# One split per q and k for both heads of a pair, with moves inside SBUF to the halves' partitions

## The chip, the core and the metric

The kernel runs on one core of a Trainium2 chip. The metric is the device time of one execution in microseconds (us); the time before is the median of three runs. The core's engines are TensorE (PE, whose weight loads are listed as PEld), VectorE (DVE), ScalarE (ACT), GpSimd (POOL) and SyncE (SP, which here issues the DMAs). Each works through its own queue in order and waits there for semaphores.

## The reference

Two decoder layers on x of 512 tokens by 1024, 16 heads of 64; layer 0 attends by stick-breaking, layer 1 by softmax with a forget gate, and each is followed by a gated MLP with a causal convolution of width 3. Cut to what matters here:

```python
for i in range(2):
    mod = silu(c) @ w_mod[i] + b_mod[i]          # six vectors: shift, scale, gate, twice
    h = rmsnorm(x, g_mix_pre[i]) * (1 + sc_a) + sh_a
    q, k, v = split_heads(h @ w_qkv[i])          # 16 heads of 64
    if i % 2 == 0:                               # strictly causal, s < t
        z = q @ k.T / 8
        a[t, s] = sigmoid(z[t, s]) * prod(1 - sigmoid(z[t, j]) for s < j < t)
    else:                                        # causal, s <= t
        a = softmax(q @ k.T / 8 + sum(log_sigmoid(f_j) for s < j <= t))
    x = x + gt_a * rmsnorm((a @ v) @ w_o[i], g_mix_post[i])
    h = rmsnorm(x, g_ffn_pre[i]) * (1 + sc_f) + sh_f
    y = (silu(conv3(h @ w_gate[i])) * (h @ w_up[i])) @ w_down[i]
    x = x + gt_f * rmsnorm(y, g_ffn_post[i])
```

## The kernel before

Everything is float32, and each matmul operand is kept as two parts: `hi`, the value rounded to the matmul's float32r format, and `lo`, what the rounding left. A product is three matmuls, hi by hi, hi by lo and lo by hi (`mm3`, lines 266 to 268, in the order ah by bh, ah by bl, al by bh). A split is a copy to hi on ACT (line 192) and a subtraction on DVE or POOL (line 193).

An attention layer works on pairs of heads, 0 to 7. `proj` makes one pair's q (j = 0) or k (j = 1): 24 matmuls into one PSUM bank with head A of the pair on partitions 0 to 63 and head B on 64 to 127. It is a generator that yields after every three matmuls; such a step is called a group here. `queries` then makes two tiles, qa and qb: qa has A's hi on rows 0 to 63 and A's lo on rows 64 to 127; qb has B's hi on 64 to 127 and B's lo on 0 to 63. Each takes one ACT and one DVE operation on 64 partitions. `keys` makes for each head a tile kh with its hi on both halves and a tile kl with its lo on its own half and zeros on the other (a fill on POOL). Per head that is an ACT copy, a POOL copy to the other half, a DVE subtraction and the fill. Two matmuls then give the three products of a score (`scores`, line 380), and since the contraction always runs over 128 rows the zeros are needed.

`attention` goes through the 16 heads. For a head it writes four score blocks and their softmax or stick-breaking (`fox`: fx, cum; `stick`: bt, om), and for the head before the transposes (pa, then ah and al) and the product with v (po). Between these it runs other matmul groups from a list, `gens`, so many per head as the table `UNITS` says: the projections of pairs 1 to 7 in order, q then k; after an even pair the four v blocks of the next two pairs (`values`, tile pv, two weight tiles of four d each); last the first products with w_o (`project`, tile po, by pair p). The PE and SP queues are in program order. The orders on ACT, DVE and POOL outside layer 0's start are set by the framework's scheduler from its own estimates, and they are fixed before the run.

Weights come through `Stream`: `need` at a projection's start also issues the next tiles, two ahead. A tile is loaded to wf (three buffers), copied to wh on ACT and subtracted to wl on POOL (three buffers each). So the load of tile i + 2 is written in SP's queue at the start of projection i, behind all that was written there before, and a DMA whose semaphore isn't there yet holds up those behind it. In layer 0, `bg.step` writes up to three loads of w_mod (tile wm) at the end of a head; DVE sums them into acc (line 143). In layer 1 each head loads a tile cum.

Of the kernel before, what the change touches and what calls it, by code (L numbers as in the profile page):

```python
# [8 lines left out]
F32 = mybir.dt.float32  # L9
F32R = mybir.dt.float32r  # L10
BF16 = mybir.dt.bfloat16
AF = mybir.ActivationFunctionType
ALU = mybir.AluOpType
AX = mybir.AxisListType

P = 128
D = 1024
S = 512
# [19 lines left out]
def trunk(ctx, tc, x, c, w_mod, b_mod, g_mix_pre, g_mix_post, w_qkv, w_o, w_fg, b_fg,  # L38
          g_ffn_pre, g_ffn_post, w_gate, w_up, w_conv, b_conv, w_down, out):
    nc = tc.nc  # L40
    cst = ctx.enter_context(tc.tile_pool(name="cst", bufs=1))
    sb = ctx.enter_context(tc.tile_pool(name="sb", bufs=1))
# [4 lines left out]
    def nm(s):  # L47
        serial[0] += 1
        return f"{s}_{serial[0]}"

    def bank(s="b"):
        return pp.tile([P, 512], F32, tag="bank", name=nm(s), bufs=8)

    def slot(s, dt=F32R):
        return sb.tile([P, 512], dt, tag="slot", name=nm(s), bufs=NS)

    def t2(s):
        return sb.tile([P, 512], F32, tag="t2", name=nm(s), bufs=4)

    def t4(s, dt=F32):  # L60
        return sb.tile([P, D], dt, tag="t4", name=nm(s), bufs=3)
# [25 lines left out]
    xs = cst.tile([P, NT, D], F32, name="xs")  # L87
    csil = cst.tile([P, ND], F32, name="csil")
    rowsA, rowsB, rowsC = t2("rowsA"), t2("rowsB"), t2("rowsC")
    nc.sync.dma_start(rowsC[:ND, :P], c.rearrange("b (r p) -> (b r) p", p=P))  # L90
    nc.scalar.dma_start(rowsA[:96, :P], b_mod.rearrange("l (r p) -> (l r) p", p=P))
# [23 lines left out]
    def conv_columns():  # L115
        ps = bank("pcol")
        for l in range(DEPTH):
            nc.tensor.transpose(ps[:, P * l : P * l + 88], rowsB[:88, P * l : P * l + P], idn[:88, :88])
        for l in range(DEPTH):
            nc.vector.tensor_copy(colB[l], ps[:, P * l : P * l + 88])  # L120
        yield
# [69 lines left out]
    def split(hi, lo, src, engine=None):  # L191
        nc.scalar.copy(hi, src)  # L192
        (engine or nc.vector).tensor_tensor(lo, src, hi.bitcast(F32), op=ALU.subtract)  # L193
# [70 lines left out]
    def mm3(ps, lhs, rhs, first, last):  # L264
        (ah, al), (bh, bl) = lhs, rhs
        nc.tensor.matmul(ps, ah, bh, start=first, stop=False)  # L266
        nc.tensor.matmul(ps, ah, bl, start=False, stop=False)  # L267
        nc.tensor.matmul(ps, al, bh, start=False, stop=last)  # L268
# [21 lines left out]
    def new_ht():  # L290
        hi = sb.tile([P, ND, S], F32R, tag="hth", name=nm("hth"), bufs=1)
        lo = sb.tile([P, ND, S], F32R, tag="htl", name=nm("htl"), bufs=1)
        return hi, lo

    def block(ht, d, c0, c1):
        return ht[0][:, d, c0:c1], ht[1][:, d, c0:c1]
# [15 lines left out]
    def modulated(t, xn, ht, gcol, shcol):  # L312

        ts_ = slice(t * P, (t + 1) * P)
        for h in range(2):
            ps = bank("pt")
            for j in range(4):
                d = 4 * h + j
                nc.tensor.transpose(ps[:, j * P : (j + 1) * P], xn[h][:, j * P : (j + 1) * P], idn)
            hf = t2("hf")  # L320
            for j in range(4):
                d = 4 * h + j
                js = slice(j * P, (j + 1) * P)
                nc.scalar.activation(hf[:, js], ps[:, js], AF.Identity, scale=gcol[:, d : d + 1], bias=shcol[:, d : d + 1])
            hi, lo = (x_[:, 4 * h : 4 * h + 4, ts_] for x_ in ht)
            hf = hf.rearrange("p (b k) -> p b k", b=4)
            (nc.scalar.copy if h else nc.vector.tensor_copy)(hi, hf)
            nc.vector.tensor_tensor(lo, hf, hi.bitcast(F32), op=ALU.subtract)  # L328

    def postnorm(t, banks, gt):  # L330
        ms, us = [square(b) for b in banks], []
        for h in range(2):
            us.append(t2("u"))
            nc.vector.tensor_tensor(us[h], banks[h], gt[:, 512 * h : 512 * h + 512], op=ALU.mult)
        r = rstd(ms)
        for h in range(2):
            x_ = xs[:, t, 512 * h : 512 * h + 512]
            nc.vector.scalar_tensor_tensor(x_, us[h], r, x_, op0=ALU.mult, op1=ALU.add)


    def proj(l, p, j, ht, scale, res, parts=((0, S),)):
        wh, wl = ws.need((l, "qk", p, j))
        ps = bank("pqk")
        for c0, c1 in parts:
            for d in range(ND):
                ds_ = slice(d * P, (d + 1) * P)
                mm3(ps[:, c0:c1], (wh[:, ds_], wl[:, ds_]), block(ht, d, c0, c1), d == 0, d == ND - 1)
                if c1 - c0 == S or d % 2:
                    yield
        res[p, j] = queries(ps, scale) if j == 0 else keys(ps)  # L350

    A, B = slice(0, HD), slice(HD, P)

    def queries(ps, scale):

        res = slot("qa"), slot("qb")
        for x_, own, other in ((res[0], A, B), (res[1], B, A)):
            nc.scalar.activation(x_[own], ps[own], AF.Copy, scale=scale)
            nc.vector.scalar_tensor_tensor(x_[other], ps[own], scale, x_[own].bitcast(F32), op0=ALU.mult, op1=ALU.subtract)
        return res  # L360

    def keys(ps):


        res = []
        for own, other in ((A, B), (B, A)):
            hi, lo = slot("kh"), slot("kl")
            nc.gpsimd.memset(lo.bitcast(F32)[other], 0.0)
            nc.scalar.copy(hi[own], ps[own])
            nc.gpsimd.tensor_scalar(hi[other], hi[own].bitcast(F32), 1.0, 1.0, op0=ALU.mult, op1=ALU.mult)  # L370
            nc.vector.tensor_tensor(lo[own], ps[own], hi[own].bitcast(F32), op=ALU.subtract)
            res.append((hi, lo))
        return res

    def scores(l, hd, qb, q, k):
# [65 lines left out]
    def values(l, g, t, ht, vt):  # L441

        w = [ws.need((l, "v", g, i), 2 - i) for i in range(2)]
        ps = bank("pv")
        for d in range(ND):
            c = slice(256 * (d % 4), 256 * (d % 4) + 256)
            mm3(ps[:, :256], block(ht, d, t * P, (t + 1) * P), (w[d // 4][0][:, c], w[d // 4][1][:, c]), d == 0, d == ND - 1)
            if d % 2:
                yield
        keep_values(ps[:, :256], g, t, vt)  # L450
# [109 lines left out]
    def begin(vt, qk):  # L560
# [169 lines left out]
        for j in range(ND):  # L730
# [16 lines left out]
            for i in order[lead:]:  # L747
                multiply(j, i)
        qk[0, 0] = queries(acc[4], 0.125)
        qk[0, 1] = keys(acc[6])  # L750
        ws.upto(1)
        for g in range(2):
# [6 lines left out]
    for l in range(DEPTH):  # L759
        bg = Background([(l, GT_A), (l, SC_F), (l, SH_F)] if l == 0 else [])  # L760
        scale = -0.125 if l % 2 else 0.125
        vt, qk = {}, {}
        if l == 0:
            with tc.manual_schedule(engines={mybir.EngineType.Activation, mybir.EngineType.DVE, mybir.EngineType.Pool}):
                ht = begin(vt, qk)
            conv_rows()
        else:
            drain(values(l, 0, 0, ht, vt))
            ready(2)
            drain(values(l, 0, 1, ht, vt))  # L770
            first = proj(l, 0, 0, ht, scale, qk, ((0, 256), (256, 512)))
            for _ in range(4):
                next(first)
            ready(3)
            drain(values(l, 0, 2, ht, vt))
            if l % 2:
                cums_of[l] = forget(ht)
            drain(values(l, 0, 3, ht, vt))
            drain(first)
            drain(proj(l, 0, 1, ht, None, qk))  # L780
# [11 lines left out]
                    mm3(banks[t][h], (ot[p][0][:, ts_], ot[p][1][:, ts_]), w[h], p == 0, p == NPAIR - 1)  # L792
                    yield

        gens, ot = [], []
        for p in range(1, NPAIR):
            if (l, p) == (0, 3):
                gens.append(conv_columns())
            gens += [proj(l, p, j, ht, s, qk) for j, s in ((0, scale), (1, None)) if (p, j) not in qk]
            if p % 2 == 0 and (p // 2, 0) not in vt:  # L800
                gens += [values(l, p // 2, t, ht, vt) for t in range(NT)]
        gens += [project(t, ps_) for ps_ in (range(3), range(3, 5)) for t in range(2)] + [project(2, range(3))]
# [6 lines left out]
        ht = new_ht()  # L809
# [77 lines left out]
        if not last:  # L887
            ht = new_ht()
# [47 lines left out]
```

## Time and profile before

| what | value |
|---|---|
| median of 3 runs | 1315.79 us (1315.13 to 1317.24) |
| the profiled execution, its own time | 1318.06 us |
| its span, first to last instruction | 1316.3 us |
| granted TensorE clock, mean | 0.994 |
| PE, DVE, ACT, POOL busy | 1249.9, 839.5, 617.8, 292.7 us |
| layer 0's attention | about 75 to 285 us |
| layer 1's attention | about 690 to 905 us |

Rows of groups read: line, engine, operation, result<-sources with partitions by elements, count | busy time, mean ns of one | idle time of the engine ahead of them and what ended it. Rows in order of time read: start in us, duration in us, engine (SPq is the DMA issue queue of SP), line, operation, and in brackets the idle time before. Rows of waits read: who, for whom, us in total, times, the longest. Rows of DMA issues end with the median us from issue to landing. Rows of stretches read: from and to, length, busy us of each engine with its count of instructions, clock, busy share of the 16 DMA engines, GB/s.

### The profile page before, as it was taken

Reading aid. Unit: us, or ns where it says so; the run is one execution under the profiler, and the core shown is the slowest. Engines: PE = TensorE matmul, PEld = TensorE weight load, DVE = VectorE, ACT = ScalarE, POOL = GpSimd, SP = SyncE. Lnnn points to the kernel's source line nnn. Section 1 sums busy time; section 2 is a strip of 40 time slices with the busy share of each in tenths; the row PEclk is TensorE's granted clock in tenths of the full one; section 3 lists DMA queues with packets and bytes.
Section 4 is the critical chain, followed back from the end, with each engine's and each line's share of the span. In section 5 each row is a group of like instructions: output and inputs, shape, how many; then the busy total and the mean of one; then the engine's idle time right before and its main releaser. Section 6 shows DMA issues by size and latency. Waiting matters only on the chain.

```text
span 1316.3 us, 17089 instructions
## 1 busy us (share of the span) xinstructions
PE 1249.9 (95%) x6244; PEld 1047.3 (80%) x6244; DVE 839.5 (64%) x1455; ACT 617.8 (47%) x1182; POOL 292.7 (22%) x326
## 2 busy tenths in 40 slices
PE   4887978999999999999999899999999999999997
PEld 3676956878888788888888789887898888888886
DVE  7979899757869898532345677786776444443233
ACT  5465655657434343321346556666753333332121
POOL 3575454641000000000032745454100000000000
PEclk9999999999999999999999999999999999999999
DMA  8653343222658777333411533432254333333221
GB/s 272 196 164 109 115 157 129 65 80 64 215 159 272 220 227 238 108 96 97 144 50 32 180 109 94 119 112 81 80 177 134 99 100 98 97 97 96 96 96 64
DMA packets 174856, 169.19 MB, mean 129 GB/s; under 512 B 6936, under 2 KB 151728, under 8 KB 174772
## 3 DMA queue, kind: packets, MB, share of 16 engines
q1 hardware_dynamic: 174596, 168.04, 41.0%
q8 instruction: 49, 0.80, 0.2%
q14 instruction: 35, 0.29, 0.1%
q10 hardware_dynamic: 176, 0.07, 0.0%
HBM read 165.92 MB, written 2.16 MB: 128 GB/s over the span
## 4 chain that ended last, share of the span: by engine, by line
PE 67%; DVE 18%; ACT 6%; DMA 4%; issue 4%; POOL 1%; SPq 1%; DVEq 0%; POOLq 0%; ACTq 0%
PE pgu L267 11%; PE pgu L268 11%; PE pgu L266 11%; PE pd L266 6%; PE pd L268 6%; PE pd L267 6%; PE pqk L266 2%; DVE om L389 2%; PE pqk L267 2%; PE pqk L268 2%; DVE acc L143 2%; PE ps L380 2%; DVE bt L390 1%; ACT junk L287 1%; PE pa L412 1%
## 5 line engine op out<-in xcount | busy, mean ns | idle before, releaser
L192 ACT CAST wh<-wf 128x1024 fp32r<-128x1024 f32 (+2 forms) x178 | 185.0, 1039 | 308.7 <-PE pd L268 134.8
L193 DVE TENSOR_TENSOR wl<-wf,wh 128x1024 fp32r<-128x1024 f32 x122 | 149.3, 1224 | 216.8 <-ACT wh L192 214.6
L267 PE MATMUL pgu<-htl,wh 128*128 128x512 f32 (+1 forms) x736 | 276.4, 376 | 0.3 <-DVE htl L328 0.2
L266 PE MATMUL pgu<-hth,wh 128*128 128x512 f32 (+1 forms) x736 | 276.4, 375 | 0.0
L268 PE MATMUL pgu<-hth,wl 128*128 128x512 f32 (+1 forms) x736 | 276.2, 375 | 0.0
L193 POOL TENSOR_TENSOR wl<-wf,wh 128x1024 fp32r<-128x1024 f32 (+3 forms) x56 | 135.2, 2418 | 230.8 <-ACT wh L192 218.6
L267 PEld LDWEIGHTS pgu<-htl,wh 128*128 128x128 f32 x736 | 138.5, 188 | 25.8 <-DVE htl L328 0.7
L266 PEld LDWEIGHTS pgu<-hth,wh 128*128 128x128 f32 x736 | 138.5, 188 | 25.0
L268 PEld LDWEIGHTS pgu<-hth,wl 128*128 128x128 f32 x736 | 138.5, 188 | 24.9
L279 POOL TENSOR_TENSOR r<-v,mhalf 128x1 f32<-128x1 f32 x32 | 17.8, 555 | 450.7 <-DVE v L275 450.7
L268 PE MATMUL pd<-wh,yl 128*128 128x512 f32 x288 | 112.0, 389 | 0.0
L266 PE MATMUL pd<-wh,yh 128*128 128x512 f32 x288 | 112.0, 389 | 0.0
L267 PE MATMUL pd<-wl,yh 128*128 128x512 f32 x288 | 112.0, 389 | 0.0
L143 DVE SCALAR_TENSOR_TENSOR acc<-wm,csil,acc 128x1024 f32<-128x1024 f32 x74 | 100.4, 1357 | 15.2 <-DMA wm<-in_w_mod_dram 14.6
L266 PE MATMUL pqk<-hth,wh 128*128 128x512 f32 (+1 forms) x240 | 100.6, 419 | 0.0
L268 PE MATMUL pqk<-hth,wl 128*128 128x512 f32 (+1 forms) x240 | 93.4, 389 | 1.1 <-POOL wl L193 1.1
L267 PE MATMUL pqk<-htl,wh 128*128 128x512 f32 (+1 forms) x240 | 93.4, 389 | 0.0
L848 ACT ACTIVATE cv<-cv 128x512 f32<-128x512 f32 x44 | 27.8, 632 | 106.1 <-DVE cv L847 100.7
L266 PE MATMUL pv<-wh,hth 128*128 128x256 f32 (+1 forms) x224 | 70.4, 314 | 0.3
L268 PE MATMUL pv<-wh,htl 128*128 128x256 f32 (+1 forms) x224 | 67.6, 302 | 1.2 <-DVE htl L662 1.0
L267 PE MATMUL pv<-wl,hth 128*128 128x256 f32 (+1 forms) x224 | 67.3, 300 | 0.0
L849 DVE TENSOR_TENSOR cv<-cv,pgu 128x512 f32<-128x512 f32 x44 | 30.2, 686 | 51.8 <-PE pgu L268 45.7
(193 smaller groups left out, 2518.6 us busy)
## 6 DMA issues: line engine op xcount, KB each, us to landing
wm<-in_w_mod_dram SPq DMA_DIRECT2D x80, 512.0 KB, 5.1
wf<-in_w_ffn_gate_dram SPq DMA_DIRECT2D x44, 512.0 KB, 4.4
wf<-in_w_ffn_up_dram SPq DMA_DIRECT2D x44, 512.0 KB, 3.6
wf<-in_w_ffn_down_dram SPq DMA_DIRECT2D x44, 512.0 KB, 3.5
wf<-in_w_qkv_dram SPq DMA_DIRECT2D x41, 512.0 KB, 3.7
wm<-in_w_mod_dram SPq DMA_DIRECT2D x32, 256.0 KB, 4.0
wf<-in_w_o_dram SPq DMA_DIRECT2D x16, 512.0 KB, 3.5
cum<-cumd SPq DMA_DIRECT2D x16, 512.0 KB, 4.3
```

Source lines behind the costliest of these rows:

```text
L143: nc.vector.scalar_tensor_tensor(acc, w, csil[:, d : d + 1], acc, op0=ALU.mult, op1=ALU.add)
L192: nc.scalar.copy(hi, src)
L193: (engine or nc.vector).tensor_tensor(lo, src, hi.bitcast(F32), op=ALU.subtract)
L266: nc.tensor.matmul(ps, ah, bh, start=first, stop=False)
L267: nc.tensor.matmul(ps, ah, bl, start=False, stop=False)
L268: nc.tensor.matmul(ps, al, bh, start=False, stop=last)
L279: nc.gpsimd.tensor_tensor(r, v, mhalf, op=ALU.pow)
L287: nc.scalar.activation(junk(), src, AF.Square, scale=1.0 / 32.0, accum_out=m)
L380: nc.tensor.matmul(ps[:, :n], q[hd][:, qs], k[hd][i][:, :n], start=i == 0, stop=i == 1)
L389: nc.vector.tensor_tensor_scan(om[:, :n][:, ::-1], ps[:, :n][:, ::-1], zid[:, S - n :][:, ::-1], 0.0, op0=ALU.mult, op1=ALU.add)
L848: nc.scalar.activation(a, a, AF.Silu)
L849: nc.vector.tensor_tensor(a, a, u, op=ALU.mult)
```

## The change

For pairs 1 to 7 (in layer 0 the q of pair 1 was made before) a q or k is split once for both heads, on all 128 partitions, into two tiles hi and lo of the four-buffer kind t2. Then DMAs on SP's queue bring their halves into place: for k six (hi to both halves of each kh, lo to the own half of each kl), for q four. The zero halves of kl are filled once per layer, in two pairs of tiles that pairs use in turn (`low_rooms`). `queries` and `keys` stay for pair 0 and for what layer 0's start makes.

```diff
-    def t2(s):
-        return sb.tile([P, 512], F32, tag="t2", name=nm(s), bufs=4)
+    def t2(s, dt=F32):
+        return sb.tile([P, 512], dt, tag="t2", name=nm(s), bufs=4)
...
-    def proj(l, p, j, ht, scale, res, parts=((0, S),)):
+    def proj(l, p, j, ht, scale, res, parts=((0, S),), kl=None):
...
-        res[p, j] = queries(ps, scale) if j == 0 else keys(ps)
+        if p:
+            res[p, j] = placed(ps, scale, kl[p % 2] if j else None)
+        else:
+            res[p, j] = queries(ps, scale) if j == 0 else keys(ps)
...
+    def placed(ps, scale, kl):
+        hi, lo = t2("hi", F32R), t2("lo", F32R)
+        def place(dst, src):
+            nc.sync.dma_start(dst.bitcast(F32), src.bitcast(F32))
+        if kl:
+            split(hi, lo, ps)
+            res = [(slot("kh"), kl[0]), (slot("kh"), kl[1])]
+            for own, (h_, l_) in zip((A, B), res):
+                place(h_[A], hi[own])
+                place(h_[B], hi[own])
+                place(l_[own], lo[own])
+        else:
+            nc.scalar.activation(hi, ps, AF.Copy, scale=scale)
+            nc.vector.scalar_tensor_tensor(lo, ps, scale, hi.bitcast(F32), op0=ALU.mult, op1=ALU.subtract)
+            res = slot("qa"), slot("qb")
+            for x_, own, other in ((res[0], A, B), (res[1], B, A)):
+                place(x_[own], hi[own])
+                place(x_[other], lo[own])
+        return res
+
+    def low_rooms():
+        res = []
+        for _ in range(2):
+            res.append((slot("kl"), slot("kl")))
+            for x_, other in zip(res[-1], (B, A)):
+                nc.gpsimd.memset(x_.bitcast(F32)[other], 0.0)
+        return res
...
-        gens, ot = [], []
+        gens, ot, kl = [], [], low_rooms()
...
-            gens += [proj(l, p, j, ht, s, qk) for j, s in ((0, scale), (1, None)) if (p, j) not in qk]
+            gens += [proj(l, p, j, ht, s, qk, kl=kl) for j, s in ((0, scale), (1, None)) if (p, j) not in qk]
```

The order of PE's instructions is the same before and after. Lines behind `proj` move down by 36. Three places show what else moves.

SP's queue at the end of layer 1's attention, before (w_o tiles o0 to o4 in order, and cum of the heads):

```order
L198 DMA wf_8556<-in_w_o_dram 128x1024
L490 DMA cum_8586<-cumd 128x1024
L198 DMA wf_8679<-in_w_o_dram 128x1024
L490 DMA cum_8718<-cumd 128x1024
L198 DMA wf_8784<-in_w_o_dram 128x1024
L198 DMA wf_8825<-in_w_o_dram 128x1024
```

The same place after (qa, qb and kh, kl are pair 7's; wf_8747 is o1, wf_8852 is o2):

```order
L384 DMA qa_8741<-lo_8738 64x512
L384 DMA qb_8742<-hi_8737 64x512
L384 DMA qb_8742<-lo_8738 64x512
L198 DMA wf_8747<-in_w_o_dram 128x1024
L526 DMA cum_8786<-cumd 128x1024
L384 DMA kh_8842<-hi_8838 64x512 x2
L384 DMA kl_6714<-lo_8839 64x512
L384 DMA kh_8843<-hi_8838 64x512 x2
L384 DMA kl_6715<-lo_8839 64x512
L198 DMA wf_8852<-in_w_o_dram 128x1024
L198 DMA wf_8893<-in_w_o_dram 128x1024
```

The loads of o2 and of the tiles after it now stand behind the six moves of pair 7's k, and that of o1 behind the four of its q. The same holds in layer 0.

SP's queue at the v weights of pairs 4 and 5 in layer 1 (two tiles of 128x4x256), before:

```order
L198 DMA wf_7358<-in_w_qkv_dram 128x8x128
L198 DMA wf_7447<-in_w_qkv_dram 128x4x256
L490 DMA cum_7468<-cumd 128x1024
L198 DMA wf_7564<-in_w_qkv_dram 128x4x256
L490 DMA cum_7607<-cumd 128x1024
```

After (qa and qb are pair 4's):

```order
L198 DMA wf_7499<-in_w_qkv_dram 128x4x256
L526 DMA cum_7520<-cumd 128x1024
L384 DMA qa_7614<-hi_7610 64x512
L384 DMA qa_7614<-lo_7611 64x512
L384 DMA qb_7615<-hi_7610 64x512
L384 DMA qb_7615<-lo_7611 64x512
L198 DMA wf_7620<-in_w_qkv_dram 128x4x256
```

The second v tile now stands behind the moves of the q that was projected just before it; it is so at all five places of this kind, two in layer 0 and three in layer 1.

DVE's queue in heads 0 and 1 of layer 0, before (om and bt of head 0, kl of pair 1, acc of w_mod):

```order
L390 TENSOR_TENSOR bt_872<-bt_872,om_873 128x127
L371 TENSOR_TENSOR kl_895<-pqk_839,kh_894 64x512
L143 SCALAR_TENSOR_TENSOR acc_1176<-wm_1179,csil,acc_1176 128x1024
L371 TENSOR_TENSOR kl_901<-pqk_839,kh_900 64x512
L389 SCALAR_TENSOR_TENSOR om_923<-ps_919,zid 128x512
L193 TENSOR_TENSOR al_938<-pa_932,ah_937 128x512
L143 SCALAR_TENSOR_TENSOR acc_1176<-wm_1182,csil,acc_1176 128x1024
L389 SCALAR_TENSOR_TENSOR om_948<-ps_944,zid 128x384
L193 TENSOR_TENSOR al_962<-pa_957,ah_961 128x384
L143 SCALAR_TENSOR_TENSOR acc_1176<-wm_1185,csil,acc_1176 128x1024
```

After, from head 0's first om on:

```order
L425 SCALAR_TENSOR_TENSOR om_835<-ps_831,zid 128x512
L193 TENSOR_TENSOR lo_903<-pqk_847,hi_902 128x512
L425 SCALAR_TENSOR_TENSOR om_855<-ps_851,zid 128x384
L425 SCALAR_TENSOR_TENSOR om_868<-ps_864,zid 128x256
L426 TENSOR_TENSOR bt_867<-bt_867,om_868 128x255
L425 SCALAR_TENSOR_TENSOR om_881<-ps_877,zid 128x128
L426 TENSOR_TENSOR bt_880<-bt_880,om_881 128x127
L425 SCALAR_TENSOR_TENSOR om_931<-ps_927,zid 128x512
L193 TENSOR_TENSOR al_946<-pa_940,ah_945 128x512
L425 SCALAR_TENSOR_TENSOR om_956<-ps_952,zid 128x384
L193 TENSOR_TENSOR al_970<-pa_965,ah_969 128x384
L395 SCALAR_TENSOR_TENSOR lo_1014<-pqk_920,hi_1013 128x512
```

One subtraction (lo) stands for the two kl, and the acc steps are gone from here: the first eight stood in heads 0 to 2 and now stand in heads 3 to 5, where w_mod's loads have come behind the moves in SP's queue.

## The prediction

> **What bounds the kernel now.** I read the page first, then stretches of time over the two attention stages (the only stages the diff touches), then the waits in them, then single rows at the places where the DMA queue's order changes.
>
> ```profile
> span 1316.3 us, 17089 instructions
> ```
>
> ```profile
> core 0: us, PE busy (x) PEld busy (x) DVE busy (x) ACT busy (x) POOL busy (x), PEclk, DMA share, GB/s
> 75.00:128.00 53.00, 43.45 (x208) 34.30 (x207) 47.03 (x67) 33.45 (x73) 31.61 (x40) 0.97 0.48 151
> 128.00:180.00 52.00, 46.19 (x279) 40.42 (x279) 47.72 (x68) 31.02 (x70) 26.24 (x38) 0.97 0.41 132
> 180.00:260.00 80.00, 70.21 (x392) 58.98 (x391) 70.77 (x130) 49.24 (x108) 41.04 (x56) 0.98 0.31 100
> ...
> 690.00:905.00 215.00, 207.27 (x1242) 179.19 (x1241) 157.21 (x392) 135.33 (x315) 108.12 (x96) 1.00 0.35 106
> ```
>
> The first three stretches are layer 0's attention (185 us). There PE idles 185 - 159.9 = 25.1 us while DVE is busy for 165.5 us, 89%: DVE is the bound. The last stretch is layer 1's attention: PE is busy for 96% and DVE for 73%. There PE is the bound, so each us that PE waits is a us of the run. The waits of layer 0 (75 to 260 us) agree, and the DMA queue's own (60 to 300 us) show that one waiting issue holds all behind it:
>
> ```profile
> PE ps L380 <- DVE om L389: 9.6, 5, 5.1
> ...
> SPq L139 <- PE pm L161: 28.4, 1, 28.4
> ```
>
> **The work that goes.** These groups are from 75 to 260 us:
>
> ```profile
> L371 DVE TENSOR_TENSOR kl<-pqk,kh 64x512 fp32r<-64x512 f32 x14 | 9.6, 683 | 2.1 <-ACT kh L369 1.9
> L193 DVE TENSOR_TENSOR al<-pa,ah 128x512 fp32r<-128x512 f32 x13 | 8.7, 671 | 0.1
> L369 ACT CAST kh<-pqk 64x512 fp32r<-64x512 f32 x14 | 8.1, 580 | 20.6 <-DVE kl L371 20.6
> L192 ACT CAST ah<-pa 128x512 fp32r<-128x512 f32 x13 | 7.7, 590 | 0.0
> L359 DVE SCALAR_TENSOR_TENSOR qb<-pqk,qb 64x512 fp32r<-64x512 f32 x6 | 4.2, 693 | 2.1 <-ACT qb L358 2.0
> L359 DVE SCALAR_TENSOR_TENSOR qa<-pqk,qa 64x512 fp32r<-64x512 f32 x6 | 4.1, 685 | 1.8 <-ACT qa L358 1.6
> ```
>
> An operation on 128 partitions costs what one on 64 does (671 beside 683 ns on DVE, 590 beside 580 on ACT). So each pair's k and each q lose one DVE and one ACT operation, and their one copy and one subtraction no longer take turns (ACT's 20.6 us of waiting for DVE at kh).
>
> Layer 0, DVE: 7 k by 0.683 and 6 q by 0.69 = 8.9 us of busy time, and of the 1.9 + 2.0 + 1.6 = 5.5 us in which DVE waited for ACT about half, 2.7. The upper bound is 11.6 us. The lower is 3, for DVE's order is new too (eight acc steps of heads 0 to 2 move to heads 3 to 5, where they make DVE full). I take **-8**. ACT (13 by 0.58) and POOL (two copies and, but for the four fills of a layer, two fills less per k) are cover, not path: nothing for them. Layer 1 (7 q, 7 k) sheds the same from engines that aren't the bound: **-1**, between 0 and -2.
>
> **What is added: transfers in SP's queue.** Per k six moves of 128 KB, per q four: 7 by 6 + 6 by 4 in layer 0 and 7 by 10 in layer 1, 136 in all. The trace has no move inside SBUF; the nearest rows are
>
> ```profile
> wf<-in_w_qkv_dram SPq DMA_DIRECT2D x41, 512.0 KB, 3.7
> wf<-in_w_o_dram SPq DMA_DIRECT2D x16, 512.0 KB, 3.5
> out_dram<-xs SPq DMA_DIRECT2D x8, 256.0 KB, 2.0
> ```
>
> so about 2 us to land, from 1 (half the bytes) to 3.5. Their own landing is mostly covered: scores read a pair's q and k one to three heads later, except pair 7. What isn't covered is SP's order. SP reaches a weight load only after the moves written ahead of it have been issued, and these wait for hi (ACT) and lo (DVE) of the projection that has just ended. Before, SP ran far ahead of PE. Where the load is used 16 matmul groups later (16 us), the delay is hidden. It isn't in two kinds of place.
>
> **Third o tile (o2), used four groups after pair 7's k.** Layer 1 before:
>
> ```profile
> 869.87 0.33 SPq L198 DMA_DIRECT2D wf<-in_w_o_dram  x1
> 884.90 1.05 ACT L192 CAST wh<-wf 128x1024 fp32r<-128x1024 f32 x1
> 886.42 2.40 POOL L193 TENSOR_TENSOR wl<-wf,wh 128x1024 fp32r<-128x1024 f32 x1
> 889.02 0.40 PE L267 MATMUL po<-wl,oh 128*128 128x512 f32 x1
> ...
> 842.32 0.49 DVE L402 TENSOR_SCALAR fx<-fx,rc 128x512 f32<-128x512 f32 x1
> ...
> 887.31 1.80 DVE L402 TENSOR_SCALAR fx<-fx,rc 128x512 f32<-128x512 f32 x1
> 890.28 0.67 DVE L371 TENSOR_TENSOR kl<-pqk,kh 64x512 fp32r<-64x512 f32 x1
> ```
>
> The load was issued 19 us before use, its split began when pair 7's projection freed the buffer, and wl was ready at 888.82 for a matmul at 889.02: no slack. Now the load stands behind pair 7's moves. DVE's lo has the place of the kl row, done at 890.95; then four issues (kl, kh twice, kl) by 0.37 = 1.5, the load 3.5, the cast 1.05, wl 2.40: 899.4, 10.4 us after the matmul wants it. The fx row ahead of kl took 1.80 us while that wl ran on POOL, and 0.49 at 842.32 with no wl beside it; with wl gone from there lo is 1.3 earlier: **+9**. The least is hi and lo at once after the projection's end (884.9, when the wh row began): 884.9 + 0.59 + 0.67 + 1.5 + 6.95 = 894.6, +5.6; the most +10.4 and a later landing, +12. The Trainium skill, "SBUF — State Buffer", section "Who interferes with whom", says that a DVE operation in its two-port mode and GpSimd lock each other out of a shared port for a whole instruction. The two fx rows agree with it; without it the term would be +10.4.
>
> Layer 0 before:
>
> ```profile
> 256.34 2.29 DVE L390 TENSOR_TENSOR bt<-bt,om 128x127 f32<-128x127 f32 x1
> ...
> 258.63 0.67 DVE L371 TENSOR_TENSOR kl<-pqk,kh 64x512 fp32r<-64x512 f32 x1
> ...
> 261.85 0.39 PE L267 MATMUL po<-wl,oh 128*128 128x512 f32 x1
> ```
>
> 259.3 + 1.5 + 6.95 = 267.75 against 261.85: 5.9. The 2.29 us bt again lay beside o2's wl; lo comes up to 1.9 earlier: **+4** (from 2 to 7). Head 14's wait for its moved kh (2 us after lo) lies inside this stall.
>
> **Second v tile, used ten groups after a q.** Layer 1's three, with SP's issue of one of these loads, the q row whose place lo takes, and the first matmul that reads wl of the second tile:
>
> ```profile
> 774.43 0.37 SPq L198 DMA_DIRECT2D wf<-in_w_qkv_dram  x1
> 748.30 0.68 DVE L359 SCALAR_TENSOR_TENSOR qa<-pqk,qa 64x512 fp32r<-64x512 f32 x1 [0.61 <-ACT qa L358]
> 755.09 0.28 PE L267 MATMUL pv<-wl,hth 128*128 128x256 f32 x1
> 798.60 0.68 DVE L359 SCALAR_TENSOR_TENSOR qa<-pqk,qa 64x512 fp32r<-64x512 f32 x1
> 804.50 0.28 PE L267 MATMUL pv<-wl,hth 128*128 128x256 f32 x1
> 847.08 0.69 DVE L359 SCALAR_TENSOR_TENSOR qa<-pqk,qa 64x512 fp32r<-64x512 f32 x1
> 852.88 0.28 PE L267 MATMUL pv<-wl,hth 128*128 128x256 f32 x1
> ```
>
> The end of lo plus three issues (1.1), the load 3.7, the cast 1.05 and wl 2.40 is 8.25 us: ready at 757.2, 807.5 and 856.0, which is 2.1 + 3.0 + 3.1 = 8.2 late, **+8** (from 1, lo at once, to 13). Layer 0's two fall where PE waits for DVE anyway: **+1.5**, from 0 to 4. The w_mod loads behind the moves are used a head later (11 us): nothing; if that cover is gone, DVE waits in order, 1 us each.
>
> **The sum:** -8 - 1 + 9 + 4 + 8 + 1.5 = +13.5. The profiled execution took 1318.06 us (span 1316.3), 2.3 above the median of the runs, 1315.79; on it the sum gives 1331.6, on the median 1329.3. I forecast **1329**; with one or two terms at their ends, 1321 to 1337.
>
> **The rivals.** *The moves are slow.* From 256 KB in 2.0 to 512 KB in 3.5 us, 128 KB takes 0.75 us of transfer. If a queue's moves run one after the other, six take 4.5 instead of the 2.2 in which they are issued and four take 3.0 instead of 1.5, ahead of the load: 2 by 2.3, 3 by 1.5 and half of 2 by 1.5 more, 4.6 + 4.5 + 1.5 = +10.6: **1340**. For it: a move reaches half the partitions; against: the 16 DMA engines are busy for only 0.35 of the time. The Trainium skill, "SBUF — State Buffer", section "Can I just issue two DMAs to hit both halves?", holds that copies to partitions 0 and 64 serialize, one pair of them gaining 6% over a single one. No run here shows it yet.
>
> *Faster: DVE's relief decides.* If in layer 0 PE gets back half of its 25.1 us, -12.5, and lo always comes at once, the v stalls vanish (8.25 + 0.59 + 0.67 after a projection's end is within the ten groups) and o2 costs 5.6 + 2.8: **1311**. Its place is DVE's queue: it decides when lo ends 8.3 us before the tile's use. Against it: two of the three qa rows show no idle time ahead of them, so there DVE came to qa from other work, later than ACT's copy.
>
> *They cancel*, within 0.2% (2.6 us, about what a measurement of this kernel can tell from no change): o2 at its least and -11.6 in layer 0: **1316**.
>
> **How the numbers follow.** My forecast 0.58, slow moves 0.20, DVE's relief 0.12, cancelling 0.10. So faster 0.12, same 0.10, slower 0.78. From 1313 to 1343 leaves out most of the faster case and the far end of the slow one; the forecast's own range is 1321 to 1337.
>
> **What the profile after would show.** Right: DVE's busy time lower by 18 us; layer 0's stretch up to pair 7 shorter; at the end of each layer's attention one PE wait of 4 to 9 us on the wl (POOL) or wh (ACT) of an o tile; PE waits of 2 to 3 us for a v tile's wl at three places in layer 1; SP waiting for ACT and DVE at the moves. The forecast is wrong if loads land before use in spite of SP's order, if the moves take well over 2 us, or if DVE's new order in layer 0 gives back more, or less, than 8 us.

## The result

The changed kernel takes 1370.41 us (1369.43 to 1372.3), the kernel before 1316.51 beside it: ratio 1.0403, 95% interval 1.0389 to 1.0418. It is slower, as forecast, but by 54 us where the sum had 13.5, and the time lies outside the range of 1313 to 1343. The two attention stages, in the same stretches of time as before (after each loss a stretch holds less of the program):

```profile
core 0: us, PE busy (x) PEld busy (x) DVE busy (x) ACT busy (x) POOL busy (x), PEclk, DMA share, GB/s
75.00:128.00 53.00, 48.89 (x241) 39.71 (x241) 43.47 (x65) 32.91 (x73) 28.15 (x37) 0.97 0.63 172
128.00:180.00 52.00, 41.83 (x240) 34.99 (x239) 44.86 (x60) 27.18 (x62) 20.76 (x29) 0.92 0.51 169
180.00:260.00 80.00, 60.63 (x335) 50.63 (x334) 60.28 (x98) 40.02 (x85) 29.22 (x36) 0.90 0.43 132
690.00:905.00 215.00, 195.69 (x1136) 170.31 (x1135) 122.63 (x311) 113.74 (x269) 76.37 (x65) 0.96 0.42 121
```

In the first stretch PE is busy for 48.89 us with 241 matmuls where it had 43.45 with 208. Little of this lead is DVE's relief. DVE has put off the first eight acc steps: the kernel before started them between 88.5 and 116.4 us, the changed one from 113.6 us on. Where they stay in place (the run without moves below, from 86.6 to 116.7 us), PE is level with the kernel before at the table's first row (122.90 us). Then it turns: 240 matmuls instead of 279, 335 instead of 392, and the granted clock, 0.97 and 0.98 before, is 0.92 and 0.90.

PE's instructions stand in one order before and after, so each matmul can be compared with itself. How far it starts behind its time before tells where the loss is made (starts in us, from the two traces):

| matmul | before | after | behind |
|---|---|---|---|
| layer 0, the transposes of pa 405 matmuls into the run | 122.75 | 113.46 | -9.3 |
| layer 0, a pv nine matmuls ahead of the first pm | 148.40 | 144.82 | -3.6 |
| layer 0, first pm | 149.41 | 150.21 | +0.8 |
| layer 0, first pm of the second group (SC_F) | 191.48 | 203.01 | +11.5 |
| layer 0, wl of the third o tile | 261.85 | 283.99 | +22.1 |
| layer 0, the last that loses | 267.65 | 291.20 | +23.6 |
| layer 1, ahead of its first loss | 737.79 | 757.07 | +19.3 |
| layer 1, wl of the last v tile | 852.88 | 891.80 | +38.9 |
| layer 1, wl of the third o tile | 889.02 | 939.82 | +50.8 |

PE's largest waits in layer 0 (75 to 330 us; who, for whom, us in total, times, the longest) and in layer 1 (690 to 960 us):

```profile
PE pm L160 <- ACT ah L146: 16.0, 2, 11.9
PE po L464 <- DVE al L193: 5.1, 7, 1.4
PE po L266 <- ACT wh L192: 3.9, 1, 3.9
...
PE po L267 <- POOL wl L193: 1.7, 1, 1.7
...
PE po L266 <- ACT wh L192: 7.3, 1, 7.3
PE pv L267 <- POOL wl L193: 6.6, 3, 3.7
PE pv L266 <- ACT wh L192: 4.1, 2, 2.8
PE pqk L268 <- POOL wl L193: 2.3, 2, 1.7
...
PE po L267 <- POOL wl L193: 1.6, 1, 1.6
```

The waits for wh and wl of o and v tiles are those of the forecast. The largest, pm's, is not: pm are the matmuls that finish one group of w_mod (from acc by ah). How the 11.9 us come about, on SP, DVE, ACT and PE after:

```profile
170.69 0.33 SPq L139 DMA_DIRECT2D wm<-in_w_mod_dram  x1
180.55 0.47 SPq L384 DMA_DIRECT2D qa<-hi  x1
184.72 0.47 SPq L384 DMA_DIRECT2D qa<-lo  x1
...
189.88 1.10 SPq L384 DMA_DIRECT2D kh<-hi  x2
...
192.96 0.59 SPq L384 DMA_DIRECT2D kl<-lo  x1
193.60 0.59 SPq L198 DMA_DIRECT2D wf<-in_w_qkv_dram  x1
194.23 0.57 SPq L139 DMA_DIRECT2D wm<-in_w_mod_dram  x1
198.99 2.89 DVE L143 SCALAR_TENSOR_TENSOR acc<-wm,csil,acc 128x1024 f32<-128x1024 f32 x1 [4.43 <-DMA wm<-in_w_mod_dram]
201.92 1.04 ACT L146 CAST ah<-acc 128x1024 fp32r<-128x1024 f32 x1 [3.53 <-DVE acc L143]
203.01 0.79 PE L160 MATMUL pm<-ah,ones 128*128 128x512 f32 x1 [11.87 <-ACT ah L146]
```

SP issues a w_mod load at 170.69 and then stands at the moves of a q, until its projection ends and hi and lo are made (180.55, 184.72), and at those of the k behind it (189.88 to 193.55). Only then, 23.5 us after the load ahead of it, goes the group's last load. It ends DVE's wait at 198.99, and the sum, the split and the matmul follow one another. PE, which has its own fixed order, stands 11.87 us at pm, and with it everything that would have made the next q and k. Before, this matmul started at 191.48 without a wait.

The third o tile of layer 1 went the way of the forecast:

```profile
927.41 1.11 SPq L384 DMA_DIRECT2D kh<-hi  x2
929.96 0.46 SPq L384 DMA_DIRECT2D kl<-lo  x1
930.52 1.19 SPq L384 DMA_DIRECT2D kh<-hi  x2
931.76 0.59 SPq L384 DMA_DIRECT2D kl<-lo  x1
932.44 1.50 SPq L198 DMA_DIRECT2D wf<-in_w_o_dram  x3
936.30 1.04 ACT L192 CAST wh<-wf 128x1024 fp32r<-128x1024 f32 x1 [3.76 <-DMA wf<-in_w_o_dram]
937.39 0.80 PE L266 MATMUL po<-wh,oh 128*128 128x512 f32 x1 [7.26 <-ACT wh L192]
939.82 0.79 PE L267 MATMUL po<-wl,oh 128*128 128x512 f32 x1 [1.64 <-POOL wl L193]
940.41 0.63 PE L268 MATMUL po<-wh,ol 128*128 128x512 f32 x1
```

Its load is issued at 932.44, behind the six moves; the first matmul with wh waits 7.3 us, that with wl another 1.64. And one thing more is to be read there: the matmuls behind the wait take 0.63 us, where the row of the kernel before, at 889.02, has 0.40. The clock is halved, which is the second part that the forecast did not have. The trace's clock records show half clock for 71.7 us after (in 11 stretches of 3.4 to 13.7 us) and 13.7 before (4 of 3.4), the end of the run aside; PE worked in 46.0 and 13.0 of them. At full clock the 33 us more would have taken half as long, so some 16.5 us are lost there; PE's busy time grew by about as much (17.5 us, from 1249.9 to 1267.4) with the same 6244 matmuls.

### The profile page after: what moved, and what is told of

Read it like the earlier page. It is cut to its first block, busy times and chain, and to the rows that moved or that the text cites. A ratio compares the mean times of both kernels' runs of the same rounds, so it can differ in the third digit from the quotient of the medians.

```text
span 1367.6 us, 17291 instructions
## 1 busy us (share of the span) xinstructions
PE 1267.4 (93%) x6244; PEld 1059.9 (77%) x6244; DVE 817.6 (60%) x1428; ACT 606.4 (44%) x1155; POOL 263.2 (19%) x278
## 4 chain that ended last, share of the span: by engine, by line
PE 69%; DVE 11%; DMA 6%; ACT 5%; issue 3%; SPq 2%; POOL 2%; DVEq 0%; POOLq 0%; ACTq 0%
PE pgu L267 12%; PE pgu L268 12%; PE pgu L266 12%; PE pd L268 5%; PE pd L267 5%; PE pd L266 5%; DMA wm<-in_w_mod_dram 2%; DMA wf<-in_w_qkv_dram 2%; PE ps L416 2%; PE pqk L268 2%; PE pqk L266 2%; PE pqk L267 2%; POOL wl L193 1%; PE pa L448 1%; DVE acc L143 1%
## 5 line engine op out<-in xcount | busy, mean ns | idle before, releaser
L143 DVE SCALAR_TENSOR_TENSOR acc<-wm,csil,acc 128x1024 f32<-128x1024 f32 x74 | 104.7, 1415 | 18.8 <-DMA wm<-in_w_mod_dram 17.9
L193 DVE TENSOR_TENSOR al<-pa,ah 128x128 fp32r<-128x128 f32 (+3 forms) x128 | 60.5, 477 | 19.8 <-ACT ah L192 19.4
```

Source lines behind the costliest of these rows:

```text
L143: nc.vector.scalar_tensor_tensor(acc, w, csil[:, d : d + 1], acc, op0=ALU.mult, op1=ALU.add)
```

## The experiments

Twelve runs tell apart the layers, the relief, the order of SP's queue, the clock and the issuing queue; two more settle a price and try a version. Each time is the median of the run beside the kernel before, on the same chip (1316.4 to 1317.9 us).

**One layer alone.** `if p:` in `proj` became `if p and l == 0:` and `if p and l == 1:`.

> The change in layer 0 alone; layer 1 splits per head as before. The lag of PE's 1126th matmul behind the same one of the kernel before, read from the two traces, is 23.6 us at the end of layer 0's attention and 19 to 22 us until layer 1's attention begins. If the two layers add, 1337 us (1333 to 1341). If instead the clock in layer 1 depends on what layer 0 left behind, the two runs of one layer each do not add up to 54.

> The change in layer 1 alone. From the lag (19.3 us at the first loss in layer 1, 51.4 at the end of its attention): 1316.5 + 32 = 1348 us (1345 to 1352).

Measured: 1337.26 and 1348.28 us, 19.9 and 30.9 above the kernel before, 50.8 together of 53.9. The lag read from the two traces gave both to about a microsecond beforehand; the layers add, to within the noise of two such runs.

**The relief without the moves.** A score reads the pair's hi and lo as they are; the run leaves out the 136 moves, and its results are therefore other ones.

```diff
-        hi, lo = t2("hi", F32R), t2("lo", F32R)
+        hi, lo = slot("hi"), slot("lo")
...
+            res = [(hi, lo), (hi, lo)]       # for a k, in place of the six moves
...
+            res = hi, lo                     # for a q, in place of the four
```

> The split once for both heads, no moves: a score reads hi and lo of the pair as they are, so its products are other ones, of the same size. Leaves out the 136 moves only. Theory: layer 0 gains what DVE was relieved of. The lag after was -9.3 us before the first wait for w_mod, over the first three heads or so; carried on over the rest of layer 0 -10 to -20, in layer 1 about -1: 1301 us (1295 to 1308). Rival (DVE's new order costs as much as its relief brings): 1312 to 1318.

Measured: 1305.16 us, ratio 0.9907 (0.9888 to 0.9925), 12.2 faster. PE is ahead by 8.3 us at the end of layer 0's attention (264.11 before, 255.80 here) and by 12.65 at the end of layer 1's (892.01, 879.36). So the forecast's first term, -8, has the right size (-8.3); layer 1's -1 was too small (-2.8 in the trace, outside its range of 0 to -2). In this run the acc steps keep their place in heads 0 to 2, so it doesn't test the order that the changed kernel has. The moves, with all that they hold up and with that order, cost 1370.4 - 1305.2 = 65 us.

**Loads ahead of the moves.** One line ahead of `placed` in `proj`:

```diff
         if p:
+            ws.upto(ws.keys.index((l, "qk", p, j)) + 3)
             res[p, j] = placed(ps, scale, kl[p % 2] if j else None)
```

> All moves stay, but at the end of each q or k projection the load of the next weight tile is written ahead of the moves instead of behind them. Theory (the order of SP's queue holds the loads back): the waits for wh and wl of o and v tiles in both layers go, with the half clock behind them, about 17 us of o tiles and 17 of v tiles and 6 of the first q in layer 1; the waits of pm for w_mod in layer 0 stay (about 20 us with their clock): 1332 us (1325 to 1345). Rival (the moves are slow or load the DMA engines): the waits stay, over 1360.

Measured: 1344.80 us, 25.6 less than the changed kernel, at the upper end of what was expected. All 136 moves are still made, so it is their place in SP's queue that costs these 25.6 us. PE has no wait for wh or wl of a v tile left in either layer; pm's stay (9.1 us for the longest), as expected. Not all of the third o tile's went: in layer 1

```profile
905.64 0.39 SPq L198 DMA_DIRECT2D wf<-in_w_o_dram  x1
908.02 1.70 SPq L385 DMA_DIRECT2D kh<-hi  x2
912.44 1.04 ACT L192 CAST wh<-wf 128x1024 fp32r<-128x1024 f32 x1 [3.37 <-DMA wf<-in_w_o_dram]
913.54 0.50 PE L266 MATMUL po<-wh,oh 128*128 128x512 f32 x1 [2.28 <-ACT wh L192]
```

the load is now ahead of the k's moves, but SP came to it late, behind the q's, and ACT waited for its landing until 912.44, 6.8 us after its issue instead of 3.5.

**Pair 7 as before.** `if p:` became `if 0 < p < NPAIR - 1:`.

> As the changed kernel, but pair 7's q and k are split per head as before, without moves. Theory (the third o tile is late because its load stands behind pair 7's k moves): the lag of 7.2 us with its clock in layer 0 and of 11.2 in layer 1 goes, and the 1.2 of head 14's wait for its moved kl; some 1 us of DVE comes back: -18, 1352 us (1347 to 1358). Rival (o2 is late for another reason): 1366 to 1372.

Measured: 1351.63 us, -18.8. The matmul with the third o tile's wl, layer 1, waits for nothing:

```profile
924.49 0.40 PE L266 MATMUL po<-wh,oh 128*128 128x512 f32 x1
924.92 0.50 PE L267 MATMUL po<-wl,oh 128*128 128x512 f32 x1
```

**pm one head later on PE.** In `mod_part`, for the three groups of layer 0's attention:

```diff
+        if l == 0 and comp in (GT_A, SC_F, SH_F):
+            for _ in range(3):
+                yield
         for h in range(2):
             cs = slice(512 * h, 512 * h + 512)
             ps = bank("pm")
```

> As the changed kernel, but in layer 0 the matmuls pm that finish a group of w_mod stand one head (three background steps) later on PE; w_mod's loads of the next groups come a head later too. Theory (pm waits because the last w_mod load of its group stands in SP's queue behind a q's and a k's moves): the two waits of 4.1 and 11.9 us go, with 1.5 of al and some 3 of half clock, less what DVE's bound gives anyway: -16, 1354 us (1347 to 1362). Rival (DVE is late by itself, and pm only shows it): the wait goes elsewhere, 1366 to 1374.

Measured: 1352.07 us, -18.3; none of these pm waits any more. The late w_mod load costs these 18 us because pm has a fixed place on PE, and DVE is not late by itself. The edit also puts the next groups' w_mod loads a head later, so the 18 us hold that too.

**Both mends.**

> Both mends on the changed kernel: loads of weight tiles ahead of the moves, pm one head later. If SP's order has two separate costs (weight tiles 25.6 us, w_mod 18.3 us), they add: 1370.4 - 43.9 = 1326.5 us (1321 to 1333). If taking away one only uncovers the other, or DVE's bound takes the room: 1335 to 1344.

Measured: 1332.46 us: -37.9, not quite the sum of 43.9, inside the interval named for adding. What remains is 16 us above the kernel before and 27 above the split alone. By PE's lag behind the split alone, 18 of the 27 have come about by 690 us and 9 come in layer 1's attention. Part of it is seen in ACT's waits of layer 0 (75 to 290 us):

```profile
ACT wh L195 <- DMA wf<-in_w_qkv_dram: 10.5, 4, 6.3
...
ACT sh L195 <- DMA wf<-in_w_o_dram: 6.7, 1, 6.7
```

The orders on ACT and DVE were fixed with loads assumed in time. A load that lands late stops the cast of its tile, and behind it on ACT the copies and products that PE and DVE need next; in the kernel before, ACT waits for no load in this stage. The longest of these waits can be followed: ACT waits 6.28 us for a load and casts its tile at 155.86, copies `of` behind it, DVE has waited 6.71 us for that copy at 157.54, and PE 5.36 us for DVE at 158.28. That such chains make up the whole remainder was not tried; the acc steps, now in heads 3 to 5, are a rival that no run here tests.

**PE kept busy while it waits.** Matmuls whose result is overwritten were put ahead of the first two pm and of the third o tile's first matmul:

```diff
+            if h == 0:
+                for _ in range({(0, GT_A): 10, (0, SC_F): 28}.get((l, comp), 0)):
+                    nc.tensor.matmul(ps, ones, ht[0][:, 0, :], start=True, stop=True)
...
+                if (t, p) == (0, 2):
+                    banks[1] = [bank("po"), bank("po")]
+                    for _ in range(20 if l else 10):
+                        nc.tensor.matmul(banks[1][0], ot[1][0][:, ts_], old[0][0], start=True, stop=True)
```

> As the changed kernel, plus matmuls without use where PE waits longest, so that it waits working: 10 and 28 ahead of the first two pm of layer 0, 10 (layer 0) and 20 (layer 1) ahead of the first matmul of the third o tile. The waits stay as long. Theory (a wait of some 3 us or more halves PE's clock for 3.4 to 13.7 us after it): the half clock at 147.7, 195.5, 280.8 and 932.7 us goes, the matmuls behind run at 375 instead of 750 ns: the lag at these four places grew by 2.5, 2.5, 1.5 and 2.3 us in the ten matmuls behind each wait; -9, 1362 us (1357 to 1367). Rival (the clock follows something else): 1368 to 1376.

Measured: 1372.41 us, no gain. The useless matmuls were too few: one takes 0.24 us from start to start, not the 0.4 of its row, so 5.5 us of the longest wait were left idle, and the clock was halved behind them all the same. So once more, with 17 and 52, 16 and 32:

> As keep_warm, with more of the useless matmuls: in keep_warm one took 0.24 us of PE, start to start, so that 5.5 us of the longest wait were left. Now 17 and 52 ahead of the two pm, 16 and 32 ahead of the third o tile. Theory (PE's clock is halved by its own idle time): the half clock at 147.7, 195.5, 280.8 and 932.7 us goes; PE was busy for 3.8 + 5.6 + 4.4 + 3.9 = 17.7 us at half clock there, of which half comes back, less what the last useless matmul overshoots: -8, 1362 us (1358 to 1368). Rival (the clock follows something else): the half clock stays and the time is 1369 to 1376.

Measured: 1362.98 us, 7.4 less than the changed kernel, although PE does 117 matmuls more. Stretches of the changed kernel around the second group's pm and layer 1's third o tile:

```profile
195.00:209.00 14.00, 5.52 (x14) 4.13 (x15) 6.83 (x12) 3.85 (x5) 2.84 (x2) 0.52 0.22 74
932.00:943.00 11.00, 3.97 (x9) 2.79 (x10) 0.66 (x3) 3.81 (x7) 5.58 (x4) 0.53 0.82 269
```

The same two places of this run, the first in two rows, and the end of the second wait:

```profile
196.00:207.00 11.00, 10.24 (x49) 8.00 (x48) 8.42 (x14) 4.27 (x8) 3.46 (x4) 1.00 0.01 2
206.00:218.00 12.00, 12.00 (x65) 10.13 (x64) 8.19 (x22) 6.88 (x15) 2.65 (x8) 1.00 0.51 150
918.00:935.00 17.00, 15.07 (x65) 11.87 (x64) 6.12 (x21) 7.43 (x18) 9.53 (x7) 0.92 0.63 201
...
929.42 0.50 PE L269 MATMUL po<-wh,oh 128*128 128x512 f32 x1
931.85 0.50 PE L270 MATMUL po<-wl,oh 128*128 128x512 f32 x1 [1.93 <-POOL wl L196]
...
932.44 0.63 PE L269 MATMUL po<-wh,oh 128*128 128x512 f32 x1
```

The clock (third number from the end) is 0.52 where PE idles and 1.00 where it is kept at work; in the last stretch a wait of 1.9 us remained, and 3.4 us at half clock behind it. PE's own idling halves its clock: keeping it at work at four places gave back 7.4 us. The Trainium skill, "TensorE: Matmul & The Clock Gate", section "What's actually happening", says that the array's clock falls to half after an idle window of some 3.4 us. The stretches of half clock here are whole multiples of 3.4 us, which agrees with that length. The condition does not: a wait of 1.9 us was enough in the last rows, and the measurement decides. Cut into steps of 3.41 us that follow on from the clock records, the run's two ends aside, the changed kernel's trace shows more. While the clock was full, each step in which PE idled for 1.47 us or more in all was followed by half clock, and none with 1.43 us or less was. In this trace several short waits within one step thus did what one long wait does; in the other traces the border lies between 1.42 and 1.84 us.

**Another queue for the moves.** `nc.sync` in `place` became `nc.scalar`, then `nc.gpsimd`.

> The same moves, issued on ACT's queue instead of SP's; all loads keep SP's queue to themselves. Theory (the loss is SP's order): the waits of PE for wh, wl and pm go, and the half clock behind them; ACT pays 136 issues of some 0.4 to 0.6 us and waits 0.7 us for each lo, 50 to 90 us of 760 it has free: 1325 us (1308 to 1340). Rival (the transfers themselves, their time or their load on the DMA engines, make the loss): 1355 to 1375.

> The same moves on POOL's queue. Theory: SP's loads are free again, but POOL makes wl and the products bt of layer 0, and each of its issues and its waits for hi and lo stands ahead of one: better than on SP, worse than on ACT: 1340 us (1318 to 1360). Rival (the transfers themselves): 1355 to 1375.

Measured: 1349.27 us on ACT, worse than expected, and 1327.96 on POOL, inside its interval; the expected order of the two came out reversed. In both, SP's loads are in time and PE's waits for pm, for v tiles and for the projections' weights are gone: those waits do not come from the transfers themselves. On ACT each issue (0.47 to 0.61 us) and each wait for lo stands ahead of work in a queue that PE waits for, so that PE waits for al, in layer 0:

```profile
PE po L464 <- DVE al L193: 14.2, 12, 6.4
```

POOL pays 0.52 us for one, and its moves land 5.0 us after it (2.3 from SP), which is late for one scores block of pair 7 and for nearly nothing else (layer 0, moves on POOL):

```profile
PE ps L416 <- DMA kh<-hi: 5.8, 1, 5.8
```

Even so this run is 22.8 us above the split alone. In layer 0 PE waits there for DVE's al (8.5 us), bt (7.6) and om (7.2); why DVE is late was not taken apart.

**Twice the moves.** The line of `place` written twice.

> As the changed kernel, each move issued twice (the second writes the same values again): 136 moves more. Theory (a move costs the 0.6 us for which SP's queue issues it, ahead of a load): each k holds what stands behind it back by 3.5 us more, each q by 2.4: third o tiles 2 by 3.5, v tiles 4 by 2.4, the last w_mod load of the long wait 6, the first q of layer 1 6, and half of that again for the clock: +25 to +35, 1400 us (1388 to 1412). If SP's issue were hidden and the waits came from hi and lo alone, 1372 (1368 to 1380).

Measured: 1598.38 us, which neither theory expected: the run does not isolate the price of an issue. SP's waits show that the second move to a place waited for the first to land:

```profile
SPq L385 <- DMA kh<-hi: 125.9, 56, 6.5
```

It says only how dear a wait in this queue is: 136 landings of 2.3 us are 313 us, and the run grew by 228. So the second transfer was sent elsewhere, to a DRAM tile of its own:

```diff
             nc.sync.dma_start(dst.bitcast(F32), src.bitcast(F32))
+            nc.sync.dma_start(dr.tile([HD, 512], F32, name=nm("spare")), src.bitcast(F32))
```

> As the changed kernel, and behind each move one more transfer of the same 128 KB, to a place in DRAM of its own that nobody reads, so that none waits for another's landing (in moves_twice each second move did, 2.3 us). Theory (a move's price is its issue on SP's queue, 0.37 to 0.6 us, ahead of a load): a k holds its load back by 2.2 to 3.6 us more, a q by 1.5 to 2.4: two third o tiles, four v tiles, the first q of layer 1, 10 issues ahead of the last w_mod load: +17 to +28, and about a fifth more for the half clock: 1395 us (1385 to 1408). If the issue were hidden and only the waits for hi and lo counted, 1372 (1368 to 1378).

Measured: 1405.18 us, +34.8, near the upper end. SP's issues of this kernel's added transfers, ns at least, median and at most:

```profile
L385 SPq DMA_DIRECT2D spare<-hi x82: 445/595/1519, 84.0 to 965.9; - x82
```

In the changed kernel, a move's issue in the same form, and its landing in us:

```profile
L384 SPq DMA_DIRECT2D kh<-hi x56: 461/587/1897, 83.3 to 931.1; - x56
...
kh<-hi SPq DMA_DIRECT2D x56, 128.0 KB, 2.4
```

A move holds SP's queue for 0.59 us. In the changed kernel PE waits 2.0 us in all for landings of moves, and ACT 2.6. So the price goes with the number of issues ahead of the loads, as the theory had it; the added transfers also write to DRAM, and what that costs was not separated.

**A version that might beat both.** The split for both heads in layer 1 alone, pairs 1 to 6, moves from POOL (`if l == 1 and 0 < p < NPAIR - 1:`, and `nc.gpsimd` in `place`).

> The version that the runs point to: the split for both heads in layer 1 alone, for pairs 1 to 6, moves on POOL's queue; layer 0 and pair 7 as before. In moves_on_pool PE's lag fell by 3.5 us over the first heads of layer 1 and then stayed until the third o tile: 1313 us (1310 to 1317), 0.25% faster than before.

Measured: 1317.37 us beside 1317.86, ratio 0.9991 (0.9979 to 1.0002): no difference that can be told. In its profiled execution PE falls behind by 3.5 us ahead of layer 1, in parts that are as before (27 us at half clock instead of 13.7), and makes up for 3.4 of it by 755 us. The gain of 3 us is seen in the trace and was not shown in the time.

## Why the prediction was wrong

The direction and the main mechanism were right: SP reaches its loads behind moves that wait for hi and lo. Two terms that the forecast put at nothing, the w_mod loads and the clock, failed. By its steps:

- *Relief, -8 and -1*: right in layer 0, where the split alone shows -8.3; too small in layer 1 (-2.8). The total is -12.2, with 1.5 us gained between the two, ahead of 600 us, where nothing was changed. What the changed kernel's own order on DVE gives or takes was not isolated.
- *Third o tile, +9 and +4*: right in kind, too small. The lag grew by 11.2 us there in layer 1 and by 7.2 in layer 0; without pair 7's moves 18.8 us went. The waits were 7.3 + 1.6 and 3.9 + 1.7; the rest is the half clock behind them.
- *Second v tiles of layer 1, +8*: the waits for wh and wl came to 6.6 + 4.1 = 10.7 us, and the half clock came on top. Layer 0's two (+1.5) came to about 1.6 us of lag each. The weights of pair 2's k in layer 1, behind pair 1's q moves (the expectations call this the first q), were not in the sum: 5.8 us by the lag. The load was used 16 groups later, where the forecast took the delay for hidden; but ACT came to that hi only at 752.67, 5 us after its projection, and head 0 runs 18 groups, not 12.
- *The issue of a move, 0.37 us*: mis-sized. It took 0.59, so a k's six hold the queue for 3.5 instead of 2.2 us.
- *"The w_mod loads behind the moves are used a head later (11 us): nothing"*: the step that failed most, 18.3 us by pm_later. The cover was reckoned for one load behind one set of moves. The last load of a group came behind a q's and a k's, 23.5 us after the load ahead of it. And the price named for a lost cover, 1 us each on DVE, looked at the wrong engine: the acc step is followed by ah and by pm, and pm has a fixed place on PE, where the wait also holds up the projection whose hi and lo SP is waiting for.
- *The clock*: left out altogether. The forecast quoted 0.97 and 0.98 for layer 0 before, and did not ask why it was below 1: three stretches of half clock, each of 3.4 us and behind PE waits. The waits of 4 to 12 us, several of which it forecast itself, brought more: some 16.5 us of lost time, by the estimate above.
- *Rivals*: slow moves has the wrong cause, since moves from POOL or behind the loads cost far less with the same transfers; but its 0.75 us for a move in the queue was nearer to the measured 0.59 than the forecast's 0.37. No run tells whether moves to the two halves hold each other up. DVE's relief does not decide, and the terms do not cancel. That last case was also mis-added: -11.6, -1, 5.6 and 2 with the v terms as forecast (8 and 1.5) make +4.5, about 1320 us, and not 1316.

So of the 65 us between the changed kernel and the split alone, 25.6 are weight tiles behind the moves and 18.3 the late w_mod group, both with the half clock that follows; together 37.9. The 18.8 us without pair 7's moves overlap with the first of these and are no further share. The other 27 are open: 18 had come about by 690 us, where at least one chain runs from a late load over ACT and DVE to PE, and 9 in layer 1.

## What to carry to other kernels

An instruction that waits for a compute result should not be put into a queue that has been running ahead with loads: every load behind it loses its lead, and the cost shows wherever another engine has a fixed place for what the load feeds. Price such a move for each thing behind it down to the last engine that waits, not to the first that reads. And reckon PE's waits with what follows them: here they brought stretches of 3.4 to 13.7 us at half clock, by estimate nearly a third of the whole loss.

## What the runs showed of the hardware

- A transfer of 128 KB inside SBUF landed 2.3 us after its issue from SP, and 5.0 after one from POOL's queue (medians). It held the issuing queue for 0.59 us from SP, 0.52 from POOL and 0.47 to 0.61 from ACT.
- A load issued right behind moves also held SP for longer: 0.57 us for the w_mod load at 194.23, 0.33 for the one at 170.69 with no move right ahead of it.
- Back-to-back matmuls of 128x512 had rows of 0.39 us and started every 0.24 us at full clock (52 of them in 12.3 us); who fills a wait with them has to count the second number.
- PE's clock fell to half for 3.4 us behind a wait of 1.9 us, and for 13.7 us around one of 11.9. In the changed kernel it fell behind each step of 3.41 us in which PE idled for 1.47 us or more, whether in one wait or in several.
